# Where the turned residual lies: a slot of its own for the rounded sums of a Strassen-style feed-forward block, and another PSUM bank for one V tile

## The chip, the cores and the metric

The kernel runs on one core of one Trainium2 chip. The metric is the time on the device in microseconds (us), the median of several runs; smaller is better. The engines that appear below are TensorE (PE; PEld is its loading of weights), VectorE (DVE), ScalarE (ACT), GpSimd (POOL) and SyncE (SP). POOL and SP issue most of the transfers (DMA).

## The reference, cut to what matters

Two layers work on one sequence of 512 tokens of width 1024. The first mixes tokens by attention over chunks, the second by a gated linear recurrence; each is followed by a feed-forward block with a squared ReLU. All of it is in float32.

```python
for layer in range(2):
    hn = rmsnorm(h, norm_mix[layer])
    h = h + (chunked_band_attention(hn, ...) if layer == 0 else rglru_block(hn, ...))
    h = h + sq_relu_mlp(rmsnorm(h, norm_mlp[layer]), mlp_w1[layer], mlp_w2[layer])
return rmsnorm(h, norm_final)

def sq_relu_mlp(h, w1, w2):            # w1: 1024 x 4096, w2: 4096 x 1024
    z = jax.nn.relu(jnp.einsum('bsd,df->bsf', h, w1))
    return jnp.einsum('bsf,fd->bsd', z * z, w2)
```

## The kernel before, in words

**Products.** Each float32 operand is split into a rounded part H and the small rest L, both in TensorE's fast float32 format. A product is then three matmuls (H with H, H with L, L with H; `mm3`, lines 287 to 290). Splitting a tile costs a rounding copy on ScalarE and a subtraction on VectorE. Weights are split the same way in `fetch` (ScalarE at line 179, VectorE at line 184), a few pieces ahead of their use. Every engine works through its own queue in order.

**Banks.** PSUM has eight banks, given to two tags of four each: `mm` (through `mmp`) and `at` (through `atp`). A tile of a tag gets a bank that an earlier tile of the tag has given up, and the first write to it waits until that earlier tile has been read.

**Attention.** At the start four projections of queries and keys (q and k of the first two pairs of heads) fill the four `mm` banks. Then the four V tiles of the first group of heads are made (`v_steps`), each in a bank of its own. A V tile is read out of its bank in two halves, each by ScalarE (line 431) and by VectorE (line 432). After that, scores (`score`, lines 483 and 484, three `at` banks for each head), their transposes (`turn` of a head) and the weighted sums alternate with the projections still to do.

**Feed-forward block** (`mlp`, once in each layer). Products are done in blocks of 2 x 2 with seven products in place of eight, with sums of blocks of weights and of inputs. `first()` starts it: four plain steps `up(0, j)`, j from 0 to 3, and then the first such group, `group(0, 1)`, which is seven pieces: `11`, `r1`, `r2`, `21`, `r3`, `22`, `r4`. The pieces `r1` to `r4` need four sums of input blocks, the right-hand sums. While the steps `up` run,

- j = 0: `turn()` turns the residual by 32 x 32 transposes on VectorE (line 744) into a tile `turned`, and 32 transfers, 16 from SP and 16 from POOL (line 751), put it into its place `d`, in which the block's output is summed;
- j = 1: ScalarE scales the residual by the norm's gain (line 697);
- j = 2: VectorE makes the four sums in place (`right`, lines 701 to 705);
- j = 3: the four sums are split (`right_split`): ScalarE rounds them into the tile `rH` (line 714), VectorE writes the rest into `rL` (line 715).

`turned` and `rH` have the same tag, `rH`, in a pool with one buffer for each tag: they share one slot of 16 KB in each partition, so the first rounding waits until the transfers out of `turned` are done.

In `group`, the bank of the first piece is copied by ScalarE to the bank that the third piece adds to (line 850); the results of the second and third piece are copied out at lines 853 and 856.

**Weights of the second matrix.** They come in blocks `11`, `12`, `22`, `21`, two loads of 512 KB each (`load_down`, line 118, on SP), into tiles with the tags `b11` and so on. `first_sum` (line 123) adds block 11 onto block 12 by two accumulating transfers from POOL. In `first()`, blocks 11 and 12 and their sum come before the steps `up`, blocks 22 and 21 after them. Loads of `kept` (line 134) bring weights for the next group; their tile takes the place of half of the residual, which the right-hand sums are read from.

**The order of the work.** The Python code gives the order in which the instructions are written. The framework that compiles it plans the order on each engine from the dependences, its own costs and the order of writing, so an instruction can be moved ahead of one that is written earlier; it also places all waits.

Of the kernel before, what the change touches and what calls it, by code (L numbers as in the profile page):

```python
# [10 lines left out]
F32 = mybir.dt.float32  # L11
F32R = mybir.dt.float32r
# [3 lines left out]
P = 128  # L16
T = 512
D = 1024
KT = D // P
NH = 16  # L20
HD = 64
U = 256
# [13 lines left out]
def f(ap):  # L36
    return ap.bitcast(F32)
# [3 lines left out]
def trunk(ctx: ExitStack, tc: tile.TileContext, xT, cols, gfin, win, wqkv, wo, rwin, rga, rgx, rwo, w1, w2, out):  # L41
# [10 lines left out]
    def mmp(name):  # L52
        return ps.tile([P, T], F32, name=name, tag="mm")
# [49 lines left out]
    def two(t):  # L103
        return t.rearrange("p (k c) -> p k c", k=2)
# [4 lines left out]
    def rows(src):  # L109
        return src.rearrange("(k p) c -> p k c", p=P)  # L110

    def load_down(key, name):
        if key not in down:
            return
        both = state["raw"].tile([P, 2, 1024], F32, name=f"b{name}_{key[0]}{key[1]}", tag=f"b{name}")
        for h in range(2):
            raws[name, h] = both[:, h]
            nc.sync.dma_start(two(raws[name, h]), rows(down[key][name][h * U : (h + 1) * U]))

    def first_sum(key):  # L120
        if key in down:
            for h in range(2):
                G.dma_start(raws["12", h], raws["11", h], accum_op=ALU.add)
# [14 lines left out]
    def fetch():  # L138
        i = state["next"]
        state["next"] += 1  # L140
        kind, nk, key = plan[i]
        H = wsp.tile([P, 1024], F32R, name=f"wh{i}", tag="wh")
        L = wsp.tile([P, 1024], F32R, name=f"wl{i}", tag="wl")
# [34 lines left out]
        if i:  # L178
            high = S.copy(H[:, :n], raw[:, :n])  # L179
            if kind in ("us1", "us3", "t1", "t4") or kind in ("t2", "t3") and key[1] == 3:  # L180
                tc.keep_in_program_order(high)
        else:
            start_.append(V.tensor_copy(H[:, :n], raw[:, :n]))
        low = V.tensor_sub(L[:, :n], raw[:, :n], f(H[:, :n]))  # L184
        if not i:
# [24 lines left out]
        elif kind == "t4" and half:  # L210
            first_sum(following)
            load_down(following, "22")
            load_down(following, "21")
        state["ready"].append((nk, H[:, :n].rearrange("p (k c) -> p k c", k=nk), L[:, :n].rearrange("p (k c) -> p k c", k=nk)))

# [4 lines left out]
    def want(n):  # L220
        prefetch(n + state["ahead"])
        got = [state["ready"].pop(0) for _ in range(n)]
        nk = got[0][0]
        return (lambda k, c: got[k // nk][1][:, k % nk, c]), (lambda k, c: got[k // nk][2][:, k % nk, c])
# [62 lines left out]
    def mm3(acc, WH, WL, XH, XL, start, stop, more=False):  # L287
        PE.matmul(acc, WH, XH, start=start, stop=False, skip_group_check=more)  # L288
        PE.matmul(acc, WH, XL, start=False, stop=False, skip_group_check=more)  # L289
        PE.matmul(acc, WL, XH, start=False, stop=stop, skip_group_check=more)  # L290
# [75 lines left out]
    with ExitStack() as actx:  # L366
# [48 lines left out]
        def v_steps(g):  # L415
            WH, WL = want(4)
            for i in range(2):
                pool, tag = (per, f"hx{i}") if g == 0 else (ab, f"v{i}")
                vt[2 * g + i] = pool.tile([P, 4, 2, 4, HD], F32R, name=f"v{2 * g + i}", tag=tag)
            c = slice(0, T)  # L420
            for t in range(4):
                acc = (atp if g == 0 and t < 2 else mmp)(f"v{g}{t}")
                ts_ = slice(t * P, (t + 1) * P)
                for k in range(KT):
                    mm3(acc, hnH[k][:, ts_], hnL[k][:, ts_], WH(k, c), WL(k, c), k == 0, k == KT - 1)
                    yield 2
                for i in range(2):
                    av = acc[:, i * U : (i + 1) * U].rearrange("p (j h d) -> p j h d", j=2, h=2)
                    v = vt[2 * g + i]
                    outer, inner = v[:, t, :, 0:4:2, :], v[:, t, :, 1:4:2, :]  # L430
                    S.activation(outer, av, AF.Copy, scale=rt[:, t : t + 1])
                    V.scalar_tensor_tensor(inner, av, rt[:, t : t + 1], f(outer), ALU.mult, ALU.subtract)
# [248 lines left out]
    def mlp(ly, norm):  # L681
        with ExitStack() as mctx:
            sr, zp, dp = (mctx.enter_context(tc.tile_pool(name=f"{n}{ly}", bufs=1)) for n in ("sr", "z", "d"))
# [2 lines left out]
            xs = [(hnH[k], hnL[k]) for k in range(KT)]  # L686
            res = dp.tile([P, 4, 2, T], F32, name=f"d{ly}", tag="d")
            dt = {(t, c): res[:, t, c] for t in range(4) for c in range(2)}
            turned = zp.tile([P, 2, 2, 4, KT, 32], F32, name=f"turned{ly}", tag="rH")
            rights = []  # L690
            rL13 = zp.tile([P, 2, 4, U], F32R, name=f"rL13{ly}", tag="rL")
            low_, high = hB[0], hB[1]
            rF = {1: low_[:, :, LO], 3: low_[:, :, HI], 4: high[:, :, LO], 2: high[:, :, HI]}
            rL = {1: rL13[:, 0], 3: rL13[:, 1]}
# [10 lines left out]
                    V.scalar_tensor_tensor(rF[n], rF[1 if n == 2 else 2], -1.0, rF[n], ALU.mult, ALU.subtract)  # L705

            def right_split(n):
                if n == 1:
                    rights.append(zp.tile([P, 4, 4, U], F32R, name=f"rH{ly}", tag="rH"))
                if n == 2:  # L710
                    rL24 = per.tile([P, 2, 4, U], F32R, name=f"rL24{ly}", tag="hx0")
                    rL.update({2: rL24[:, 0], 4: rL24[:, 1]})
                H = rights[0][:, n - 1]
                S.copy(H, rF[n])  # L714
                V.tensor_sub(rL[n], rF[n], f(H))  # L715

            def operand(n):
                if n[0] == "r":
                    H, L = rights[0][:, int(n[1]) - 1], rL[int(n[1])]
                    return [(H[:, k], L[:, k]) for k in range(4)]  # L720
                ks, c = (range(4) if n[0] == "1" else range(4, KT)), (LO if n[1] == "1" else HI)
                return [(hnH[k][:, c], hnL[k][:, c]) for k in ks]
# [15 lines left out]


            def turn():  # L740
                blocks = [turned[:, h] for h in range(2)]
                for k in range(KT):
                    for h in range(2):
                        V.transpose(
                            blocks[h].rearrange("p t j k a -> p (t j) k a")[:, :, k],
                            hT[k][:, h * U : (h + 1) * U].rearrange("p (n b) -> p n b", b=32),
                        )
                for h in range(2):
                    for i in range(4):
                        for j in range(4):  # L750
                            (G if j % 2 else nc.sync).dma_start(
                                res[32 * j : 32 * j + 32, 2 * h : 2 * h + 2, i // 2, (i % 2) * U : (i % 2 + 1) * U],
                                blocks[h][32 * i : 32 * i + 32, :, j].rearrange("p t k a -> p t (k a)"),
                            )
# [8 lines left out]
            def up(p, j):  # L763
                WH, WL = want(1)
                acc = mmp(f"u{ly}{p}{j}")
                project([acc], [slice(0, P)], WH, WL, xs)
                for h in range(2):
                    if j % 4 == 0:
                        a[p, j // 4, h] = take(F32, f"a{p}{j // 4}{h}")
                    c = a[p, j // 4, h][:, j % 4]  # L770
                    S.activation(c, acc[:, h * U : (h + 1) * U], AF.Relu)
                    S.activation(c, c, AF.Square)
                if j == 0:
                    turn()
                if j == 1:
                    for k in range(KT):
                        scaled(k)
                if j == 2:
                    for n in (1, 3, 2, 4):
                        right(n)  # L780
                if j == 3:
                    for n in (1, 3, 2, 4):
                        right_split(n)
# [10 lines left out]
            def first():  # L794
                state["kept"] = sr.tile([P, 2, 1024], F32, name=f"kept0{ly}", tag="b21")
                load_up((ly, 0), "s1")
                load_up((ly, 0), "22")
                load_down((ly, 0), "11")
                load_down((ly, 0), "12")
                first_sum((ly, 0))  # L800
                for j in range(4):
                    up(0, j)
                state["kept"] = per.tile([P, 2, 1024], F32, name=f"kept{ly}", tag="hx1")
                load_up((ly, 1), "s1")
                here = group(0, 1)
                next(here)
                opening(0)
                load_down((ly, 0), "22")
                for n in range(5):
                    next(here)  # L810
                load_down((ly, 0), "21")
                load_up((ly, 1), "22")
                next(here)
                sums(0, False)
                sums(0, True)
                lengths()
# [265 lines left out]
    def open_x(u):  # L1082
        WH, WL = want(1)
        for i in range(2):
            xbs.append(mmp(f"xb{2 * u + i}"))
            project(xbs[-1:], PAIR[i : i + 1], WH, WL, [(hnH[k], hnL[k]) for k in range(4, KT)], last=False)
            yield

    mlp(0, nm1)


    nm2 = Norm("nm2", C_MLP1, late=True)
    with ExitStack() as rctx:
# [83 lines left out]
        for u in range(4):  # L1177
            WH, WL = want(2 if u > 1 else 1)
            for i in range(2):
# [3 lines left out]
                acc = xbs[c] if c < 4 else (atp if c == 4 else mmp)(f"xb{c}")  # L1183
# [52 lines left out]
        for u in range(2, 4):  # L1236
            WH, WL = want(2)
            for i in range(2):
                m = 2 * u + i
                project([accs[m]], PAIR[i : i + 1], WH, WL, [gd[k] for k in range(KT)])  # L1240
                ro_out(m)

    mlp(1, nm2)


# [39 lines left out]
```

## Time and profile before

| | |
|---|---|
| Runs, us | 1032.22, 1033.96, 1036.42 |
| Median, us | 1033.96 |
| Profiled execution, us | 1035.93 |
| Its span, us | 1034.2 |
| Mean granted TensorE clock | 0.999 |
| Read from HBM | 123.27 MB |

The profile is of one execution; times within it count from the start of the span. A row of a timeline has the start, the duration, the engine, the line of the code, the operation, what it writes and reads, and how many instructions are merged; in brackets stands how long the engine was idle before it, and what ended that. A row of the waits has the engine and line, what it waited for, the total in us, how often, and the longest. A row of the loads gives the time from issue to landing. In the feed-forward blocks the residual's tiles are called `h` in the first layer and `t` in the second.

### The profile page before, as it was taken

The page shows a single profiled execution, that of the slowest core. Times are in us where ns is not written, and L with a number is a line of the kernel's source. Part 1 is how long each engine was busy: PE and PEld are TensorE (multiplying, and loading weights), DVE is VectorE, ACT ScalarE, POOL GpSimd, SP SyncE. Part 2 cuts the span into 40 slices and gives each one's busy share as a digit, 9 for nine tenths or more (in the row PEclk, how much of TensorE's full clock was granted, in tenths as well). Part 3 has the DMA queues.
Part 4 walks back from the last instruction along what each step waited for, and adds up shares of the span by engine and source line. Part 5 has one row for each costly group of instructions (what it writes and reads, how often), then busy time and mean ns, then how long its engine had stood idle before and what let it go on. Part 6 is the DMA issues. An engine that isn't in the chain of part 4 may idle for free.

```text
span 1034.2 us, 15261 instructions
## 1 busy us (share of the span) xinstructions
PE 1021.6 (99%) x5762; PEld 892.5 (86%) x5762; DVE 866.8 (84%) x1222; ACT 665.7 (64%) x1020; POOL 99.4 (10%) x128
## 2 busy tenths in 40 slices
PE   9999999999999999999999999999999999999997
PEld 7888888888999999999988788888899999999986
DVE  7998778869789898698688989977789698698687
ACT  7676556646787566567567686645786567567565
POOL 1000000003101111111020000012101111111020
PEclk9999999999999999999999999999999999999999
DMA  8444344249648738828773412196648838828572
GB/s 269 120 124 140 84 153 121 74 121 247 173 79 232 208 56 216 218 51 214 205 143 102 123 62 82 43 281 167 159 90 225 217 57 211 223 49 212 142 166 84
DMA packets 125482, 153.62 MB, mean 149 GB/s; under 512 B 6497, under 2 KB 94561, under 8 KB 125409
## 3 DMA queue, kind: packets, MB, share of 16 engines
q1 hardware_dynamic: 102752, 114.18, 35.2%
q0 software_dynamic: 22080, 37.76, 21.1%
q8 instruction: 45, 0.74, 0.3%
q10 hardware_dynamic: 576, 0.72, 0.2%
q14 instruction: 29, 0.23, 0.1%
HBM read 123.27 MB, written 2.10 MB: 121 GB/s over the span
## 4 chain that ended last, share of the span: by engine, by line
PE 82%; DVE 7%; DMA 5%; ACT 2%; SPq 2%; issue 1%; DVEq 0%; ACTq 0%
PE m L289 9%; PE m L288 9%; PE m L290 9%; PE x L288 6%; PE x L289 6%; PE x L290 6%; PE y L288 4%; PE y L289 4%; PE y L290 4%; DVE wl L184 2%; PE x L514 1%; PE v L288 1%; DMA wr<-in_w 1%; PE v L290 1%; PE yb L290 1%; PE v L289 1%
## 5 line engine op out<-in xcount | busy, mean ns | idle before, releaser
L184 DVE TENSOR_TENSOR wl<-b,wh 128x1024 fp32r<-128x1024 f32 x112 | 135.6, 1221 | 31.4 <-ACT wh L179 31.2
L179 ACT CAST wh<-b 128x1024 fp32r<-128x1024 f32 x112 | 116.7, 1051 | 57.7 <-PE x L290 18.8
L289 PE MATMUL m<-rL,wh 128*128 128x256 f32 x448 | 126.2, 282 | 0.9 <-DVE rL L715 0.9
L288 PE MATMUL m<-rH,wh 128*128 128x256 f32 x448 | 126.1, 281 | 1.0 <-ACT rH L714 0.6
L290 PE MATMUL m<-rH,wl 128*128 128x256 f32 x448 | 125.9, 281 | 0.0
L179 ACT CAST wh<-wr 128x1024 fp32r<-128x1024 f32 (+1 forms) x65 | 66.7, 1029 | 47.9 <-PE wo L289 11.8
L290 PE MATMUL m<-hnH,wl 128*128 128x256 f32 x336 | 95.0, 283 | 0.0
L289 PE MATMUL m<-hnL,wh 128*128 128x256 f32 x336 | 95.0, 283 | 0.0
L288 PE MATMUL m<-hnH,wh 128*128 128x256 f32 x336 | 94.9, 282 | 0.0
L184 DVE TENSOR_TENSOR wl<-wr,wh 128x1024 fp32r<-128x1024 f32 (+1 forms) x66 | 78.2, 1188 | 12.3 <-ACT wh L179 11.9
L289 PEld LDWEIGHTS m<-rL,wh 128*128 128x128 f32 x448 | 84.9, 190 | 2.8 <-DVE rL L715 1.5
L288 PEld LDWEIGHTS m<-rH,wh 128*128 128x128 f32 x448 | 84.8, 189 | 2.6 <-ACT m L850 0.8
L290 PEld LDWEIGHTS m<-rH,wl 128*128 128x128 f32 x448 | 84.9, 189 | 0.0
L179 ACT CAST wh<-u 128x1024 fp32r<-128x1024 f32 x56 | 58.0, 1050 | 25.3 <-PE x L290 16.9
L184 DVE TENSOR_TENSOR wl<-u,wh 128x1024 fp32r<-128x1024 f32 x56 | 67.6, 1219 | 2.3 <-ACT wh L179 2.3
L289 PEld LDWEIGHTS m<-hnL,wh 128*128 128x128 f32 x336 | 64.2, 191 | 0.8
L288 PEld LDWEIGHTS m<-hnH,wh 128*128 128x128 f32 x336 | 64.2, 191 | 0.8
L290 PEld LDWEIGHTS m<-hnH,wl 128*128 128x128 f32 x336 | 64.3, 191 | 0.0
L288 PE MATMUL x<-wh,h 128*128 128x512 f32 (+1 forms) x132 | 50.9, 386 | 0.6 <-DVE d L1059 0.6
L290 PE MATMUL x<-wh,l 128*128 128x512 f32 (+1 forms) x132 | 50.9, 385 | 0.0
L289 PE MATMUL x<-wl,h 128*128 128x512 f32 (+1 forms) x132 | 50.7, 384 | 0.0
L288 PE MATMUL y<-wh,hs 128*128 128x512 f32 x128 | 50.2, 392 | 0.0
(384 smaller groups left out, 2892.6 us busy)
## 6 DMA issues: line engine op xcount, KB each, us to landing
b<-in_w SPq DMA_DIRECT2D x68, 512.0 KB, 6.1
b<-b POOLq DMA_DIRECT2D x36, 512.0 KB, 7.0
kept<-in_w SPq DMA_DIRECT2D x28, 512.0 KB, 3.8
u<-in_w SPq DMA_DIRECT2D x28, 512.0 KB, 5.8
wr<-in_wqkv SPq DMA_DIRECT2D x20, 512.0 KB, 4.2
wr<-in_rwin SPq DMA_DIRECT2D x16, 512.0 KB, 3.6
kept<-in_w POOLq DMA_DIRECT2D x14, 512.0 KB, 8.1
u<-in_w POOLq DMA_DIRECT2D x14, 512.0 KB, 7.4
```

What stands on the lines that cost most here:

```text
L179: high = S.copy(H[:, :n], raw[:, :n])
L184: low = V.tensor_sub(L[:, :n], raw[:, :n], f(H[:, :n]))
L288: PE.matmul(acc, WH, XH, start=start, stop=False, skip_group_check=more)
L289: PE.matmul(acc, WH, XL, start=False, stop=False, skip_group_check=more)
L290: PE.matmul(acc, WL, XH, start=False, stop=stop, skip_group_check=more)
L514: PE.transpose(b[:, c : c + P], pt[:, seg[t] + kt * P : seg[t] + (kt + 1) * P], ident)
```

## The change

Three things, the first two of which belong together:

1. `turned` no longer takes the slot of `rH`. It becomes two tiles, one for each half of the tokens, with the tags `b22` and `b11`: they lie where blocks 22 and 11 of the second matrix are loaded later. `rH` is allocated at the start and has its slot for itself. The half in `b11` is transferred out first.
2. Blocks 22 and 11 can therefore be loaded only after the transfers out of these tiles. The load of block 11 is now written behind the step `up(0, 0)`, the sum of blocks 11 and 12 behind the four steps.
3. In attention the second V tile (t = 1) takes a bank of the tag `mm` instead of one of `at`; only the first V tile still has one of `at`.

```diff
@@ v_steps @@
-                acc = (atp if g == 0 and t < 2 else mmp)(f"v{g}{t}")
+                acc = (atp if g == 0 and t == 0 else mmp)(f"v{g}{t}")
@@ mlp @@
-            turned = zp.tile([P, 2, 2, 4, KT, 32], F32, name=f"turned{ly}", tag="rH")
-            rights = []
+            rH = zp.tile([P, 4, 4, U], F32R, name=f"rH{ly}", tag="rH")
@@ right_split @@
-                if n == 1:
-                    rights.append(zp.tile([P, 4, 4, U], F32R, name=f"rH{ly}", tag="rH"))
...
-                H = rights[0][:, n - 1]
+                H = rH[:, n - 1]
@@ turn @@
-                blocks = [turned[:, h] for h in range(2)]
+                blocks = [sr.tile([P, 2, 4, KT, 32], F32, name=f"turned{ly}{h}", tag=f"b{n}") for h, n in enumerate(("22", "11"))]
...
-                for h in range(2):
+                for h in (1, 0):
                     for i in range(4):
                         for j in range(4):
                             (G if j % 2 else nc.sync).dma_start(
@@ first @@
                 load_up((ly, 0), "s1")
                 load_up((ly, 0), "22")
-                load_down((ly, 0), "11")
                 load_down((ly, 0), "12")
-                first_sum((ly, 0))
                 for j in range(4):
                     up(0, j)
+                    if j == 0:
+                        load_down((ly, 0), "11")
+                first_sum((ly, 0))
```

More of the change, by code (lines that the diff above doesn't have):

```diff
@@ L718, in operand @@
                 if n[0] == "r":
-                    H, L = rights[0][:, int(n[1]) - 1], rL[int(n[1])]
+                    H, L = rH[:, int(n[1]) - 1], rL[int(n[1])]
                     return [(H[:, k], L[:, k]) for k in range(4)]
```

## The prediction

> **What bounds the kernel now.** I read the page first, for the engine that sets the time.
>
> ```profile
> PE 1021.6 (99%) x5762; PEld 892.5 (86%) x5762; DVE 866.8 (84%) x1222; ACT 665.7 (64%) x1020; POOL 99.4 (10%) x128
> ```
>
> TensorE has work for 99% of the span, and no other engine is near that. Time can be won only where TensorE stands still, so the second view is its waits, whole span, longest first (total, times, longest).
>
> ```profile
> PE s L483 <- issue: 1.0, 1, 1.0
> ...
> PE m L289 <- DVE rL L715: 0.9, 1, 0.9
> ...
> PE m L288 <- ACT rH L714: 0.6, 1, 0.6
> ...
> PE m L288 <- ACT m L850: 0.4, 2, 0.2
> ```
>
> Four of the few waits lie where the change is. L483 is a score product in attention. The three others are the products with the right-hand sums at the start of each feed-forward block (`group(0, 1)`). These idle times are what is left after the modelled ends of the matmuls, so I measured the loss by start times instead: TensorE's timeline in the second block (start, duration, then in brackets the idle time).
>
> ```profile
> 733.51 0.28 PE L290 MATMUL m<-hnH,wl 128*128 128x256 f32 x1
> 734.35 0.38 PE L288 MATMUL m<-rH,wh 128*128 128x256 f32 x1 [0.56 <-ACT rH L714]
> 735.61 0.39 PE L289 MATMUL m<-rL,wh 128*128 128x256 f32 x1 [0.88 <-DVE rL L715]
> 735.83 0.28 PE L290 MATMUL m<-rH,wl 128*128 128x256 f32 x1
> 735.95 0.28 PE L288 MATMUL m<-rH,wh 128*128 128x256 f32 x1
> ...
> 738.35 0.28 PE L290 MATMUL m<-rH,wl 128*128 128x256 f32 x1
> 738.83 0.38 PE L288 MATMUL m<-rH,wh 128*128 128x256 f32 x1 [0.20 <-ACT m L850]
> ...
> 739.46 0.28 PE L290 MATMUL m<-rH,wl 128*128 128x256 f32 x1
> ```
>
> An undisturbed product of 256 columns starts 0.12 us after the one before it (735.83 to 735.95). From 733.51 to 735.83 three steps take 2.32 instead of 0.36: 1.96 lost. From 738.35 to 739.46 three steps take 1.11: 0.75 lost. The second block loses 2.71 us. The same place in the first block:
>
> ```profile
> 272.35 0.28 PE L290 MATMUL m<-rH,wl 128*128 128x256 f32 x1
> 272.84 0.38 PE L288 MATMUL m<-rH,wh 128*128 128x256 f32 x1 [0.21 <-ACT m L850]
> ...
> 273.48 0.28 PE L290 MATMUL m<-rH,wl 128*128 128x256 f32 x1
> ```
>
> Three steps in 1.13 instead of 0.36: 0.77 lost. Together the two blocks lose 3.48 us.
>
> The Trainium skill (Perfetto Trace Analysis, Identifying the Most-Contended Engine) warns that the busy share of matmuls is no good measure of TensorE's distance from its limit, since pipelined matmuls look smaller than they are. The idle times above would give only 0.9 + 0.6 + 0.4 = 1.9 us for the two blocks; the trace agrees with the warning, as the starts show 3.48.
>
> **The change, part 1: a place of its own for the rounded sums.** Why does TensorE wait? ScalarE's timeline in the second block, then its one row in the first:
>
> ```profile
> 727.80 0.72 ACT L772 ACTIVATE a<-a 128x256 f32<-128x256 f32 x2
> 733.25 1.05 ACT L714 CAST rH<-t 128x1024 fp32r<-128x1024 f32 x1 [4.72 <-DMA d<-turned]
> ...
> 735.36 2.94 ACT L714 CAST rH<-t 128x1024 fp32r<-128x1024 f32 x3
> 738.19 0.59 ACT L850 COPY m<-m 128x512 f32<-128x512 f32 x1
> ...
> 742.98 1.05 ACT L179 CAST wh<-b 128x1024 fp32r<-128x1024 f32 x1
> 743.92 0.59 ACT L856 COPY u<-m 128x512 f32<-128x512 f32 x1
> ```
>
> ```profile
> 267.26 1.05 ACT L714 CAST rH<-h 128x1024 fp32r<-128x1024 f32 x1 [3.88 <-DMA u<-in_w]
> ```
>
> The cast of the first sum into `rH` is ready to go when the sums are, but `rH` takes the slot of `turned`, and the 32 transfers out of `turned` must land first. ScalarE stands 4.72 us for them, then does four casts, and the copy L850, which TensorE's third piece needs, stands behind the casts in ScalarE's queue. That is the second loss (738.35 to 739.46). In the first block the profile names another transfer, `u<-in_w`; the code gives the cast no reason to wait for that one, and the last `turned` transfer is due at the same moment, so I take the cause to be the same.
>
> The sums themselves are early. VectorE:
>
> ```profile
> 722.97 1.23 DVE L705 SCALAR_TENSOR_TENSOR t<-t 128x1024 f32<-128x1024 f32 x1
> ...
> 728.84 1.23 DVE L166 TENSOR_TENSOR u<-u,us 128x1024 f32<-128x1024 f32 x1
> ```
>
> The last sum is done at 724.20, ScalarE is free from 728.52 and VectorE from 730.07. With a slot of its own the casts need four times 0.98 (2.94 / 3): 728.5 to 732.4. The differences `rL` follow on VectorE at about 1.23 each: 730.1 to 735.0. TensorE needs the first of them at 733.7 and, without the first loss, the second sum's at 733.6 + 24 x 0.12 = 736.5; this is the third of the four in VectorE's order, done at 733.8. The copy L850 then runs as soon as its bank is full, at 733.8. What is late next is nothing in this stretch, so all 3.48 us go. The count of casts, differences, transposes and transfers stays as it was; the transposes write into the tiles of blocks 22 and 11 instead, at no cost, since nothing has used these since the layer before ended.
>
> **Part 2: blocks 22 and 11 load later.** Block 11 was loaded long before this stretch; now its load stands on SP's queue behind the 16 `turned` transfers that SP issues and must wait for the landing of those of its half (they are now issued first). SP's timeline, and the landing times of all loads of `b`:
>
> ```profile
> 716.83 12.95 SPq L751 DMA_DIRECT2D d<-turned  x16
> 740.35 0.93 SPq L134 DMA_DIRECT2D kept<-in_w  x2
> ```
>
> ```profile
> DMA to landing us min/median/max: 3.5/6.2/11.2
> ```
>
> SP is through at 729.78 and had nothing to issue until 740.35, so behind the load nothing waits on SP. Block 11 lands at 736.0 (median) or 741.0 (slowest). ScalarE wants it for L179 at 742.98, less the 2.71 won: 740.3. This costs nothing at the median with 4.3 us to spare, and at the slowest 0.7 us of ScalarE's time. Ahead of it POOL's first sum (block 12 plus 11) waits for the landing too; behind that on POOL stands only the accumulation into `kept`, which follows a load that SP issues at 740.35. Block 22 is wanted two steps of the round later than 11. Are the transfers in each other's way? This view gives busy time by engine and, at the end of the row, the share of the DMA engines and GB/s:
>
> ```profile
> 733.51:739.46 5.95, 4.29 (x29) 3.49 (x28) 5.03 (x5) 5.95 (x10) 0.00 (x0) 1.00 0.00 0
> ```
>
> In the stretch in which the moved loads would land the DMA engines moved nothing; I count zero.
>
> The Trainium skill speaks against the move (DMA: Bandwidth & Descriptors, Issuing engines are not separate DMA queues): transfers of SP and of POOL share the same 16 engines and interleave. By it the moved loads would compete with each other, with the last `turned` transfers and with POOL's accumulations, and the slowest landing would be the one to count on: 0.7 us in each of two blocks, 3.48 + 0.7 - 1.4 = 2.8 won, 1031.2 us. The row above, with its share of 0.00, speaks for the median, and I keep zero.
>
> **Part 3: the second V tile.** TensorE, ScalarE and VectorE around the score product of head 1, and the two reads that free the banks of the first projections:
>
> ```profile
> 33.86 0.39 PE L288 MATMUL v<-wh,hnH 128*128 128x512 f32 x1
> ...
> 39.30 0.39 PE L288 MATMUL v<-wh,hnH 128*128 128x512 f32 x1
> ...
> 41.26 0.40 PE L288 MATMUL v<-wh,hnH 128*128 128x512 f32 x1
> 42.61 0.30 PE L483 MATMUL s<-kl,q 128*128 128x128 f32 x1 [0.96 <-issue]
> ...
> 43.16 0.34 PE L483 MATMUL s<-kl,q 128*128 128x384 f32 x1
> ```
>
> ```profile
> 29.98 0.65 DVE L384 SCALAR_TENSOR_TENSOR tq<-qk,n0acc 128x512 f32<-128x512 f32 x1
> ...
> 36.38 0.68 DVE L384 SCALAR_TENSOR_TENSOR tq<-qk,n0acc 128x512 f32<-128x512 f32 x1
> ...
> 42.02 0.48 DVE L432 SCALAR_TENSOR_TENSOR v<-v,rt,v 128x256 fp32r<-128x256 f32 x1 [0.34 <-ACT v L431]
> 42.42 0.41 DVE L487 CUSTOM_DVE_ANT_0 p<-s,bias 128x256 f32<-128x256 f32 x1
> ```
>
> The `at` tag has four banks. In order they go to the warm-up, the norm, V tiles 0 and 1, then three scores of head 0, and the fourth score after V tile 1, the first of head 1, gets V tile 1's bank. That is read last by VectorE at 42.02, done at 42.50, and the score starts at 42.61. The step took 1.35; a 512-column step takes 0.23 in this stretch (24 of them from 33.86 to 39.30), so 1.12 is lost. After the change that score gets V tile 0's bank, free long before. But head 1's second score bank is that of head 0's first, read until 42.83 (42.42 + 0.41), where the third product of head 1 started at 43.16. If nothing fills the time up to then, only 0.33 is won; if V matmuls fill it, all of 1.12. I take 0.7, between the two, as such matmuls follow. The price is paid in the `mm` banks: V tile 1 now waits for the first q bank (read done at 30.63, product at 33.86) and V tile 2 for the second (37.06 against 39.30): 2.2 us to spare at the least, cost nothing.
>
> **The sum.** 3.48 + 0.7 = 4.2 us. The profiled execution took 1035.93 us (its span of 1034.2 and 1.7 around it) and would take 1031.7; it lies 2 us above the median of the runs shown. From that median, 1033.96, I get **1029.8 us**, 0.4% less. A measurement of this kernel can tell about 0.5% (5.2 us) from no change; the forecast is just inside.
>
> **Rivals.** *Slower: the load of block 11 ends up behind the `kept` loads.* The framework's planner, not the code, sets the order on SP. The `kept` loads wait until the last `rL` is done. Behind them the load would be issued at 741.3 and land 6.2 to 11.2 later, at 747.5 to 752.5; ScalarE's cast then waits 7 to 12 us, with the copy L856 behind it, which holds TensorE's fifth piece. It costs from the landing at 740.3 on. Two blocks: 14 to 24, less 4.2: 1044 to 1054; with the median landing 1044. Against it: the load is written before the `kept` loads and is ready 10 us earlier. *Attention keeps its wait.* The planner sees other banks and orders the scores anew; nothing is won there, and one more wait of that size arises: 3.48 - 1.12 = 2.4, or 1031.6. *The reverse*: the new order takes away all of the 1.12 and one more wait of that size: 3.48 + 2.24 = 5.7, or 1028.2. *It doesn't do what it says*: the cast in the first block waits for `u<-in_w` indeed, so 0.77 stays: 3.4, or 1030.5.
>
> **How the numbers follow.** Forecast 0.60, attention keeps its wait 0.14, the reverse 0.11, first block keeps its wait 0.08, load behind `kept` 0.07. The runs shown lie from 1032.22 to 1036.42, so a median of three can sit 1.5 us off. The three milder cases span 1028.2 to 1031.6; with that noise the range is 1026.8 to 1032.8, which leaves out the slower rival and some of the edges. Faster by over 0.5% means below 1028.8: a quarter of the forecast (0.16), most of the reverse (0.08), a few of the others (0.04), and 0.04 for a gain that I have not seen: 0.32. Slower by over 0.5%: 0.07. The rest, 0.61, is within.
>
> **What would show it.** Right: the waits of TensorE no longer list L289 on `rL`, L288 on `rH` or on L850; the casts L714 start before 730 in the second block with no wait on `d<-turned`; the loads of `b` stand on SP right behind `turned`; L483 no longer waits near 42. Wrong: a wait of ScalarE's L179 on `b<-in_w` near 740, POOL's first sum after 745, or new waits of TensorE in attention.

## The result and the profile after

The changed kernel takes 1038.2 us in the median of 11 runs (1035.87 to 1043.15); beside it the kernel before took 1034.49 (11 runs, 1032.22 to 1037.53). The ratio is 1.0037 with an interval of 1.0022 to 1.0053: slower by 0.37%, where 0.4% faster was forecast. The profiled execution took 1038.07, its span 1036.3.

TensorE's waits over the whole span, after (total, times, longest):

```profile
PE y L288 <- ACT wh L179: 2.1, 1, 2.1
PE y L289 <- DVE wl L184: 1.7, 2, 1.4
PE warm L547 <- POOL ones L87: 1.0, 1, 1.0
PE s L483 <- DVE mx L487: 1.0, 1, 1.0
```

The three waits at the right-hand sums are gone from the list, as forecast. Two new ones stand at its head: the products `y`, which multiply activations with blocks of the second matrix, wait for split weights. ScalarE's timeline, after:

```profile
252.40 2.00 ACT L711 CAST rH<-h 128x1024 fp32r<-128x1024 f32 x2
...
279.30 0.63 ACT L835 ACTIVATE a<-a 128x512 f32<-128x512 f32 x1
284.79 1.05 ACT L179 CAST wh<-u 128x1024 fp32r<-128x1024 f32 x1 [4.86 <-DMA u<-in_w]
...
295.77 2.00 ACT L179 CAST wh<-b 128x1024 fp32r<-128x1024 f32 x2
...
714.06 1.04 ACT L711 CAST rH<-t 128x1024 fp32r<-128x1024 f32 x1
...
720.69 2.94 ACT L711 CAST rH<-t 128x1024 fp32r<-128x1024 f32 x3
```

The casts into `rH` (L711 here, L714 before) come early. In the first block the first one starts at 252.40, where it stood at 267.26; in the second it starts at 714.06, where it stood at 733.25, and the other three follow at 720.69. But at 279.93 ScalarE stops for 4.86 us, because weights `u` of the next group haven't landed. Ten microseconds of small work follow, and the casts of block 12, which the first `y` needs, run at 295.77. What TensorE makes of that, with the place in attention and the second block in the same view:

```profile
40.88 0.33 PE L483 MATMUL s<-kl,q 128*128 128x256 f32 x1
41.05 0.28 PE L484 MATMUL s<-kh,q 128*128 128x256 f32 x1
42.36 0.45 PE L483 MATMUL s<-kl,q 128*128 128x384 f32 x1 [1.03 <-DVE mx L487]
...
294.46 0.28 PE L290 MATMUL m<-hnH,wl 128*128 128x256 f32 x1
296.87 0.50 PE L288 MATMUL y<-wh,hs 128*128 128x512 f32 x1 [2.13 <-ACT wh L179]
298.72 0.62 PE L289 MATMUL y<-wl,hs 128*128 128x512 f32 x1 [1.35 <-DVE wl L184]
299.14 0.63 PE L290 MATMUL y<-wh,ls 128*128 128x512 f32 x1
299.57 0.63 PE L288 MATMUL y<-wh,hs 128*128 128x512 f32 x1
300.00 0.41 PE L288 MATMUL m<-rH,wh 128*128 128x256 f32 x1
300.21 0.41 PE L289 MATMUL m<-rL,wh 128*128 128x256 f32 x1
...
302.48 0.28 PE L288 MATMUL m<-rH,wh 128*128 128x256 f32 x1
...
763.32 0.39 PE L288 MATMUL y<-wh,hs 128*128 128x512 f32 x1
764.09 0.50 PE L289 MATMUL y<-wl,hs 128*128 128x512 f32 x1 [0.38 <-DVE wl L184]
764.43 0.39 PE L290 MATMUL y<-wh,ls 128*128 128x512 f32 x1
```

By starts, with 0.12 us for a step of 256 columns and 0.23 for one of 512: from 294.46 to 299.14 three steps take 4.68 in place of 0.58, so 4.10 is lost. From 299.14 to 302.48 two wide and twelve narrow steps take 3.34 in place of 1.90: another 1.44, because each step has nearly doubled (0.43 and 0.21). The granted clock shows why; busy time by engine (PE, PEld, DVE, ACT, POOL), then the clock, the DMA engines' share (it adds up the times of the packets, and so can pass 1) and GB/s, after:

```profile
265.00:270.00 5.00, 5.00 (x38) 4.77 (x38) 3.16 (x4) 3.62 (x8) 1.13 (x2) 1.00 1.11 332
270.00:275.00 5.00, 5.00 (x44) 5.00 (x43) 3.54 (x4) 2.68 (x5) 1.92 (x2) 1.00 1.08 306
275.00:280.00 5.00, 5.00 (x44) 5.00 (x43) 2.43 (x2) 3.56 (x5) 0.00 (x0) 1.00 1.08 228
...
297.00:300.00 3.00, 1.65 (x5) 1.03 (x6) 3.00 (x6) 3.00 (x4) 0.00 (x0) 0.82 0.01 3
300.00:302.00 2.00, 2.00 (x11) 2.00 (x10) 2.00 (x2) 1.09 (x3) 0.20 (x1) 0.50 0.00 0
```

So the first block loses 5.54 where it lost 0.77 before. The second block loses 0.65 at 763.32 (1.11 in place of 0.46) where it lost 2.71. Attention loses 1.14 (41.05 to 42.36, less 0.17) where it lost 1.12. That is 4.77 - 2.06 + 0.02 = 2.7. The profiled execution after also began its V products 0.54 us earlier (27.88 against 28.42), which leaves 2.2; the spans differ by 2.1.

Why is `u` late? SP issues two loads of `u` in this block (between 270 and 280). Their times from issue to landing (least, median, most), before and then after:

```profile
DMA to landing us min/median/max: 4.5/4.7/4.9
```

```profile
DMA to landing us min/median/max: 13.5/13.7/13.8
```

What stands ahead of them on the issuing queues, after, SP first and then POOL:

```profile
249.33 11.09 SPq L748 DMA_DIRECT2D d<-turned  x16
260.73 0.90 SPq L118 DMA_DIRECT2D b<-in_w  x2
263.52 0.37 SPq L134 DMA_DIRECT2D kept<-in_w  x1
264.30 0.89 SPq L118 DMA_DIRECT2D b<-in_w  x2
265.23 0.56 SPq L134 DMA_DIRECT2D kept<-in_w  x1
271.21 1.50 SPq L134 DMA_DIRECT2D u<-in_w  x2
```

```profile
268.02 0.89 POOL L123 DMA_DIRECT2D b<-b  x1 [7.10 <-DMA b<-in_w]
269.76 0.85 POOL L123 DMA_DIRECT2D b<-b  x1 [0.85 <-DMA b<-in_w]
271.38 1.31 POOL L136 DMA_DIRECT2D kept<-in_w  x1 [0.77 <-DVE wl L184]
```

Block 11 (260.73) and block 22 (264.30) are 2 MB of new loads in this stretch, and the sum of blocks 11 and 12, two accumulating transfers of 512 KB from one tile to another, now runs at 268 to 271, just ahead of the loads of `u` at 271.21. The first of these is issued 8.7 us before ScalarE comes free for it at 279.93; a landing of 13.5 us puts it at 284.7, where the cast starts. In the kernel before, the stretch from 265 to 275 was nearly empty:

```profile
265.00:270.00 5.00, 5.00 (x36) 4.64 (x36) 1.66 (x2) 2.74 (x6) 0.00 (x0) 1.00 0.27 48
270.00:275.00 5.00, 4.76 (x38) 4.36 (x37) 4.90 (x5) 5.00 (x7) 0.00 (x0) 1.00 0.01 3
```

A DMA share of 0.27 and 0.01 there has become 1.11 and 1.08. That the moved transfers are in the way is likely from this; which of them, and whether they are the whole of the loss, the profile doesn't say. The theory to test: the moved work, above all the sum, delays `u`. The rivals: the new bank of the V tile costs the time; the late block 11 or its sum itself is missing at the products; any 2 MB of loads there would do the same; the sum costs wherever it stands.

### The profile page after: what moved, and what is told of

Same layout as the page of the kernel before. It is cut to its first block, busy times and chain, and to the rows that moved or that the text cites. A ratio compares the mean times of both kernels' runs of the same rounds, so it can differ in the third digit from the quotient of the medians.

```text
span 1036.3 us, 15286 instructions
## 1 busy us (share of the span) xinstructions
PE 1021.9 (99%) x5762; PEld 893.8 (86%) x5762; DVE 866.6 (84%) x1222; ACT 666.4 (64%) x1020; POOL 98.8 (10%) x128
## 4 chain that ended last, share of the span: by engine, by line
PE 91%; DVE 4%; ACT 2%; DMA 2%; issue 1%; DVEq 0%; ACTq 0%; POOL 0%; POOLq 0%
PE m L290 8%; PE m L289 8%; PE m L288 8%; PE x L288 5%; PE x L289 5%; PE x L290 5%; PE y L289 4%; PE y L290 4%; PE y L288 4%; PE x L514 2%; PE wo L288 1%; PE ro L290 1%; PE wo L289 1%; PE v L288 1%; PE ro L289 1%; PE wo L290 1%
## 5 line engine op out<-in xcount | busy, mean ns | idle before, releaser
L179 ACT CAST wh<-u 128x1024 fp32r<-128x1024 f32 x56 | 58.2, 1050 | 34.2 <-PE x L290 16.9
L289 PE MATMUL y<-wl,hs 128*128 128x512 f32 x128 | 50.3, 393 | 1.7 <-DVE wl L184 1.7
```

## The experiments

Each group has its own runs of the kernel before: 1034.86 for e1 to e4 (28 runs), 1034.92 for e5 to e8 (28 runs), 1035.5 for e9 to e11 (11 runs). All the results first; the last column is the time to landing of SP's two loads of `u` in the first block, in us (4.5 and 4.9 in the profile of before).

| run | median (runs) | ratio to before, interval | `u` |
|---|---|---|---|
| after | 1038.2 (11) | 1.0037, 1.0022 to 1.0053 | 13.5, 13.8 |
| e1, V tile alone | 1035.23 (12) | 1.0003, 0.9992 to 1.0015 | |
| e2, turned tiles alone | 1037.64 (10) | 1.0030, 1.0018 to 1.0041 | 13.5, 13.9 |
| e3, other places, early loads | 1032.32 (9) | 0.9973, 0.9963 to 0.9983 | 3.9, 8.7 |
| e4, e3 with the old V bank | 1032.40 (10) | 0.9973, 0.9961 to 0.9985 | 3.9, 8.7 |
| e5, only block 11 and the sum late | 1033.06 (10) | 0.9982, 0.9973 to 0.9992 | 10.7, 11.3 |
| e6, only block 22 late | 1032.30 (9) | 0.9974, 0.9964 to 0.9984 | 4.5, 7.8 |
| e7, change without the sum | 1032.38 (10) | 0.9970, 0.9959 to 0.9981 | 6.2, 7.1 |
| e8, e3 and two blocks loaded again | 1032.32 (8) | 0.9974, 0.9964 to 0.9985 | 4.1, 5.7 |
| e9, change with the sum later | 1032.59 (8) | 0.9972, 0.9961 to 0.9982 | 6.2, 7.3 |

**e1: the kernel before with the second V tile in the other bank.**

```diff
-                acc = (atp if g == 0 and t < 2 else mmp)(f"v{g}{t}")
+                acc = (atp if g == 0 and t == 0 else mmp)(f"v{g}{t}")
```

> Only the second V tile's bank is changed, all else is the kernel before. Theory (the loss sits in the first feed-forward block, the bank is harmless): 0.4 us won, since the wait of 1.0 at the score product only moves from the first to the second bank of head 1; within 0.15% of the kernel before, about 1034. Rival (the new bank order costs time further on in attention): slower by 2 us or more, with new waits of TensorE before 230 us.

No difference that can be measured. Its waits show the reason: the first score of head 1 no longer stops, the next one but one does.

```profile
PE s L483 <- DVE mx L487: 1.3, 1, 1.3
```

**e2: the change with the V tile as before.**

```diff
-                acc = (atp if g == 0 and t == 0 else mmp)(f"v{g}{t}")
+                acc = (atp if g == 0 and t < 2 else mmp)(f"v{g}{t}")
```

> Only the place of the turned residual and the later loads, the V tile as before. Theory: the whole loss is here, about 3.5 to 4 us slower than the kernel before: TensorE stands 3 to 4 us at the first products with the second weights in the first feed-forward block, after a cast of u that waits for a late load. Rival (the bank did it): as fast as the kernel before or 3 us faster.

The loss is here: 1.0030, with the same two waits of `y` (2.2 and 1.1) and the same late landing of `u`. The bank falls as the cause.

**e3: `rH` in its own slot, but the turned tiles elsewhere.** The two halves lie in the slots of `rL` (free until the differences are written) and of a pair of activation tiles that are written only later; all loads and the sum stand where they stood before. The diff is against the changed kernel; the lines that allocate the two slots are left out.

```diff
-                blocks = [sr.tile([P, 2, 4, KT, 32], F32, name=f"turned{ly}{h}", tag=f"b{n}") for h, n in enumerate(("22", "11"))]
+                blocks = [zp.tile([P, 2, 4, KT, 32], F32, name=f"turned{ly}0", tag="h12"), zp.tile([P, 2, 4, KT, 32], F32, name=f"turned{ly}1", tag="rL")]
...
+                load_down((ly, 0), "11")
                 load_down((ly, 0), "12")
+                first_sum((ly, 0))
                 for j in range(4):
                     up(0, j)
-                    if j == 0:
-                        load_down((ly, 0), "11")
-                first_sum((ly, 0))
```

> The rounded sums have a slot of their own, but the turned residual lies in slots of the feed-forward pool that are needed later (that of the rests rL and a pair of the h tiles), so blocks 11 and 22 load as early as before; the V tile as in the changed kernel. Theory (the moved loads fill the DMA engines, so the load of u lands late): the wait of ScalarE for u goes, u lands in 4 to 8 us instead of 13.5, and what was promised stays: 3.5 + 0.4 won, about 1030.5. Rival (the earlier rounding itself brings the kept loads forward into a jam): u still lands after 10 us or more and the time stays near 1037.

This has part 1 of the prediction without part 2. It wins, 1032.32, and TensorE waits neither at the sums nor at `y`. The gain is 2.5 us in the medians, not the 4 expected. `u` lands in time (3.9 and 8.7).

**e4: e3 with the V tile as before** (the line of e1 turned back).

> As the run before, but with the V tile in its old bank. Theory: 3.5 won, about 1031, 0.4 us behind the run before. Rival (the bank costs time): faster than the run before by 2 us or more.

1032.40 beside 1032.32, where about 1031 was expected: on this footing too the V tile's bank is worth nothing.

**e5 and e6: one moved block at a time.** In e5 one half of the turned tiles lies in `b11`, so block 11 and the sum come late; in e6 one lies in `b22`, and block 11 and its sum come early.

```diff
e5: +  blocks = [zp.tile(..., tag="h12"), sr.tile(..., tag="b11")]
e6: +  blocks = [sr.tile(..., tag="b22"), zp.tile(..., tag="rL")]
```

> Half of the turned residual in the tile of block 11 (loaded late, with its sum behind it), the other half in the pair of h tiles; block 22 loads early. Theory (traffic: the load of u lands 13.5 us after issue because the moved loads and the sum fill the DMA engines; free of cost up to about 9.6): 1 MB less ahead of u, it lands 3 to 4 us earlier, at about 10; TensorE loses 0 to 1 us there, time about 1032.5 to 1033.5. Rival (block 11 and its sum come too late for the products with block 12, whatever the traffic): TensorE still waits 3 to 4 us at the first y products, time 1037.

> Half of the turned residual in the tile of block 22 (loaded late), the other half in the slot of the rests rL; block 11 and its sum early. Theory: 1 MB in place of 2 MB and the sum, u lands at 7 to 10 us, no wait of TensorE, about 1032.5. Rival (it was block 22's load alone, standing between the two loads of kept on SP): u at 13 us and 1037.

ScalarE's wait for `u` in e5:

```profile
ACT wh L179 <- DMA u<-in_w: 2.8, 2, 2.3
```

Block 22 alone makes nothing wait (4.5 and 7.8). With block 11 and the sum late, `u` lands after 10.7 and 11.3, and TensorE loses one wait of 1.2 at `y`, without a fall of the clock: the kernel takes 0.8 us more than e6. Only both together make 13.5. The comparison isn't quite clean, since the sum's first transfer is issued at 265.79 in e5 and at 268.02 in the change.

**e7: the change without the two transfers of the sum.**

```diff
                 for j in range(4):
                     up(0, j)
                     if j == 0:
                         load_down((ly, 0), "11")
-                first_sum((ly, 0))
```

> The changed kernel without the two accumulating transfers that add block 11 onto block 12 at the start of each feed-forward block (so one of the seven products takes block 12 alone: part of the computation is left out). Theory: 1 MB of transfers between tiles less; u lands 2 to 4 us earlier, TensorE's wait at the first y products shrinks to 0 to 1.5 us, time 1032.5 to 1034.5. Rival (the sum is free, only loads from HBM count): u still after 13 us, 1037.

One product then takes block 12 alone, so part of the computation is left out. With both blocks still loaded late, `u` lands in time, some 7 us earlier where 2 to 4 were expected, and the whole loss is gone (1032.38).

```profile
DMA to landing us min/median/max: 6.2/6.6/7.1
```

In this kernel the stretch from 270 to 275 moved 365 GB/s, where the change moved 306. So 2 MB of plain loads issued ahead of `u` are not enough to delay it.

**e8: e3, with blocks 11 and 22 loaded a second time** behind the last of the `turned` transfers.

```diff
                 for j in range(4):
                     up(0, j)
                     if j == 0:
+                        for again in ("11", "22"):
+                            load_down((ly, 0), again, last_turned[0])
```

> The version with the turned residual in slots of its own and all loads early (1032.3), and blocks 11 and 22 loaded a second time, with the same contents, behind the transfers of the turned residual on SP. It has the traffic of the moved loads (2 MB) without a late sum and without shared tiles. Theory: u lands after 10 to 13 us in place of 7, and TensorE loses 0.5 to 4 us at the first y products of the first block, about 1033 to 1036. Rival (not traffic, but the order or the sum): u as without, 1032.3.

The 10 to 13 us for `u` didn't come: 4.1 and 5.7, and the time of e3. That agrees with e7, and the theory in its general form (any 2 MB there) falls. By itself e8 is the weaker of the two: `u` was issued at 273.18, two microseconds later than in the change, with one load of `kept` behind it, and the repeated loads, issued from 262.87, had nearly all landed by then.

**e9: the change, with the same transfers, and only the sum's two put behind POOL's accumulation into `kept`.**

```diff
-                first_sum((ly, 0))
                 state["kept"] = per.tile([P, 2, 1024], F32, name=f"kept{ly}", tag="hx1")
-                load_up((ly, 1), "s1")
+                kept_sum = load_up((ly, 1), "s1")
+                first_sum((ly, 0), kept_sum)
```

> The changed kernel, whole, with only the order on POOL changed: the two transfers that add block 11 onto block 12 come behind the accumulation into kept, so they are issued after the loads of u. Theory (the sum's transfers between tiles stand in the way of the load of u): u lands in 7 to 10 us in place of 13.5, TensorE's wait at the first y products goes or falls below 1 us, time 1032.3 to 1033.5. Rival (the sum costs wherever it stands, now as a late block 12): TensorE waits 2 us or more at the first y products, time 1036 or more.

POOL's timeline, and the landing of `u`, which SP issued at 271.38:

```profile
272.06 1.30 POOL L138 DMA_DIRECT2D kept<-in_w  x1 [10.99 <-DVE wl L186]
272.83 2.32 POOL L123 DMA_DIRECT2D b<-b  x2
```

```profile
DMA to landing us min/median/max: 6.2/6.8/7.3
```

Nothing is left out and no byte less is moved. The sum is issued 1.5 us behind the first load of `u` in place of 3.2 and 1.5 us ahead of it, and 13.5 and 13.8 become 6.2 and 7.3; the kernel takes 1032.59, by the ratios 0.65% less than the change. ScalarE casts `u` at 280.76, where the change had 284.79, and block 12 at 291.74, where it had 295.77: the whole queue stands 4.03 us earlier, which is nearly the 4.10 that TensorE lost at the first `y`. That settles three rivals: the sum doesn't cost wherever it stands, block 11, loaded at the same time as in the change, is not too late for the products, and the sum, now later still, isn't either.

**e10 and e11: the kernel before, twice more, one execution each.** No edit.

> The kernel before once more, for a second profile. Theory (a stall of about 2 us of TensorE may or may not be followed by a stretch at half the granted clock, which makes the times of this kernel spread by 5 us): the waits of TensorE at the rounded sums are the same 0.6, 0.9 and 0.2; the clock in the 3 us behind them is 1.00 or about 0.5. Rival (the spread comes from elsewhere): always 1.00, or other waits.

> As the run before this one, for a third profile: the same waits of TensorE in the second feed-forward block, the clock behind them 1.00 or about 0.5; with the half clock the later stages start 1.5 to 2 us later.

e10 (1033.98) loses 2.6 us in the second block, nearly the 2.71 of the first profile, but nothing in the first block. e11 (1035.06) loses 0.4 in the second and 0.5 in the first. ScalarE's row in e11:

```profile
732.35 1.05 ACT L714 CAST rH<-t 128x1024 fp32r<-128x1024 f32 x1 [1.46 <-DMA d<-turned]
```

The wait for the last `turned` transfer was 1.46, where the first profile had 4.72. The stall that the change was to take away isn't the same in each execution: 3.5, 2.6 and 0.9 us for both blocks. The clock stayed at 1.00 in the stretch behind it in both, so the half clock that the expectation offered for the spread of the times wasn't seen here.

## Why the prediction was wrong

**The step that failed** is part 2, "This costs nothing". It followed the moved load of block 11 to its own user (ScalarE's cast at 740.3), found 4.3 us to spare, and ended there. That much was right: no cast waited for a block. (The row of landings that it read, 3.5/6.2/11.2, takes in POOL's accumulating transfers of the whole span; the two loads of block 11 themselves landed after 6.3 and 9.1 us in the second block.) But the victim was another load, and what was counted as zero came to 5.5 us of TensorE's time in the first block. The text said of POOL that "behind that on POOL stands only the accumulation into `kept`" and of SP that behind the load nothing waits; it never asked which transfers, on any queue, are issued next and how far ahead of their use. In the first block these are the loads of `u`. Shown by experiments: they are late because of the sum standing ahead of them (e9, e7). Block 22's load adds to it (e5 against the change), as far as these two can be compared. Read from the timelines: ScalarE, which works in order, waits 4.86 us for `u`, the casts of block 12 come 4.03 us later than in e9, and TensorE stands.

**The row that misled.** The DMA share of 0.00 was that of 733.51 to 739.46 in the second block. There the kernel loses little after the change too: 0.65 us in all (and 0.6 in e9). The first block was taken to be like it, and wasn't looked at. From 265 to 275 it had been nearly as empty (0.27 and 0.01); the question was how full it would become, and who would need it. The 2 MB of the moved loads and the sum's transfers would have been countable from the code.

**The Trainium skill's rule.** The prediction weighed a rule of the Trainium skill (DMA: Bandwidth & Descriptors, Issuing engines are not separate DMA queues), by which transfers of SP and POOL interleave on the same engines, and set it aside. The trace agrees with the rule: POOL's sum delays SP's loads of `u` (13.5 and 13.8 us, against 6.2 and 7.3 in e9). The price that the prediction gave it, 0.7 us in each block, was worked out for the wrong victim; TensorE lost 5.5 in the first block and 0.65 in the second.

**Part 1 was right in its mechanism.** With a slot of their own the first casts come 14.9 and 19.2 us earlier, and all waits at the sums are gone, in both blocks. That the first block would keep its wait for `u<-in_w`, a rival, didn't happen. In e10 the same cast starts at 265.26, while the transfer of `u` that the profile names there was issued at 259.65 and landed 6.3 us later, at 265.95: the cast wasn't waiting for it. The size, 3.48, was that of one profiled execution. In the medians e3 wins 2.5 us with an interval of about 1.8 to 3.8 (0.17% to 0.37% of 1034.86), and the three profiles of the kernel before show why: 3.5, 2.6 and 0.9 us were there to win, 2.3 in the mean. So 3.48 was probably too high as a forecast for a median; the interval alone doesn't rule it out.

**Part 3 won nothing.** What came is the rival that attention keeps its wait: 1.14 in place of 1.12, and not at the bank that the V tile gave up but at head 1's second score bank. The prediction saw this bank's last read at 42.83, and took 0.7, hoping for V products to fill the time; just one stands behind the waiting score (42.82), and none ahead of it.

**The slower rival** put block 11's load behind the `kept` loads. One `kept` load did come between blocks 11 and 22 (263.52), but block 11 went ahead of it, and the price named there, a wait of ScalarE for block 11, never arose. The outcome was on the slower side by a mechanism that no rival held.

**What stays open.** Why an accumulating transfer holds up its neighbours more than a load of the same size does was not taken apart by a run. The records of the packets give part of an answer: the sum's 1 MB went in 256 packets of 4 KB that took 0.327 us each, the loads of `u` in packets of 1 KB that took 0.051 us. Shared among 16 engines that makes 5.2 us for the sum and 3.3 for 1 MB of such loads, by estimate. The sum also held up a load that was issued ahead of it: the second load of `kept` (265.23) landed after 16.9 us, in e7 after 10.7 and in e9 after 10.8. Whether `u` is late for standing beside the sum, or for standing behind that `kept` load on SP's queue, no run separates.

The kernel before spreads over 1032.1 to 1039.1 us and e3 over 1031.5 to 1032.8. Part of that is the stall, and part lies at the very start: the V products began at 27.57 in e10 and at 29.72 in e11. Those 2.15 us outweigh the 1.7 that e11 lost less at the sums, and e11 was the slower of these two. Why the start differs stays open.

**The better versions.** e3 is 0.27% under the kernel before, and e9 0.28% in its own group: the first by places that touch no load, the second by the change itself with two of its transfers moved.

## What to carry to other kernels

When a tile is moved into a slot that is loaded later, follow not only the moved load to its user: list every transfer that will be under way in the stretch into which the load falls, on all queues, those issued before it too, and ask of each how far ahead of its use it is issued. If a stage occurs twice, do this in both places, since the margins differ. And take the size of a stall from more than one execution before you forecast its removal.

## What the runs showed of the hardware

**The sum's place.** Two accumulating transfers of 512 KB between tiles, issued 3.2 and 1.5 us ahead of the first of two loads, raised the landing of these from 6.2 and 7.1 us (e7) to 13.5 and 13.8 (after), while 275 to 280 moved only 228 GB/s at a share of 1.08. Issued 1.5 us behind the first load, they left them at 6.2 and 7.3 (e9).

**The clock after short waits.** TensorE's granted clock fell to 0.50 behind waits of 2.13 and 1.35 us with one product between them (300 to 302 after). In e1 it fell behind far shorter ones, the 0.6 and 0.9 us at the sums:

```profile
734.00:737.00 3.00, 1.48 (x9) 1.21 (x9) 2.30 (x2) 3.00 (x7) 0.00 (x0) 0.96 0.00 0
737.00:740.00 3.00, 3.00 (x16) 3.00 (x15) 2.90 (x4) 3.00 (x4) 0.00 (x0) 0.50 0.00 0
```

Beside it the first profile of before, with nearly the same waits and a clock that stays up, as it did in e10:

```profile
737.00:740.00 3.00, 2.77 (x21) 2.37 (x20) 2.90 (x3) 3.00 (x5) 0.00 (x0) 1.00 0.00 0
```

In these 3 us e1 has 16 products recorded, before 21. The Trainium skill (TensorE: Matmul & The Clock Gate, HAM oscillation — how this bites in real kernels) warns of idle gaps of TensorE over some 3.4 us. The changed kernel's two waits come to 3.5 together; the 1.5 us of e1 is less than half of that and was followed by the half clock, while nearly the same waits in the profile of before and in e10 were not. So by these runs idle time shorter than the figure can cost clock too, though not each time. What it adds is 1.44 us to 4.10 in the changed kernel.
